# A Mamba-2 and HGRN2 trunk: SSD chunks in backs and fronts, silu as one operation, the last tiles squared in two steps

## The chip, the cores and the metric

The kernel runs on one core of a Trainium2 chip. The metric is the device time of one execution in microseconds (us). The core's engines are PE (matrix products and transposes), DVE (vectors), ACT (functions of single elements, copies), POOL (little used here) and SP (which issues transfers). Each takes its instructions in a fixed order and waits on semaphores for the others.

## The reference

One step of a trunk of two layers for 1024 new frames and 32 frames of a running stream, with 1024 channels. The first layer is an SSD mixer, the second an HGRN2 mixer, and each is followed by a SwiGLU network; every part begins with an RMS norm, and one ends the whole. The change touches the first norm, the SSD mixer and the last norm. Of the mixer:

```python
def ssd_mixer(h, conv_buf, ssm_state, in_w, conv_w, conv_b, dt_bias, A_log, D_skip, gnorm_w, out_w):
    proj = h @ in_w
    z = proj[..., :SSD_D_INNER]
    xbc = proj[..., SSD_D_INNER:SSD_D_INNER + SSD_CONV_DIM]
    dt_raw = proj[..., SSD_D_INNER + SSD_CONV_DIM:]
    ...
    xbc = jax.nn.silu(acc)          # acc: causal convolution of xbc over 4 frames
    ...
    y, S = ssd_scan(xs, dt, A, Bm, Cm, ssm_state.astype(jnp.float32))
    y = y + D_skip.astype(jnp.float32)[:, None] * xs
    yg = y.reshape(Bsz, L, SSD_D_INNER) * jax.nn.silu(z.astype(jnp.float32))
    yg = yg * lax.rsqrt(jnp.mean(yg * yg, axis=-1, keepdims=True) + NORM_EPS)   # over groups of 512
    ...
    out = yg.astype(h.dtype) @ out_w
```

The scan goes over chunks of frames. With the decay from frame s to frame t of a chunk, it adds (C_t . B_s) x decay x dt_s x_s over s (the chunk's own part) to C_t . S x decay (the part of the state S), and then carries S on.

## The kernel before

Frames are columns, channels are the 128 partitions. The 1056 frames are worked on as two halves, h = 0 (512 frames) and h = 1 (544, with the running stream's 32 at the end). All products in f32 are made of three: a weight tile "raw" is split into wh (ACT copy, L118) and wl (DVE, raw minus wh, L121), and `product` (L346 to L348) multiplies wh by the input's high part, wh by its low part, and wl by its high part, for each of eight tiles of channels. So PE's third matmul of a product needs wl.

The SSD layer runs over eight units (h, g), g being one of four groups of eight heads. For a unit, `conv_tile` makes six tiles: a product into an "mm" bank of PSUM (one of 512 columns in the first half, two of 272 in the second), the bias copy "pre" on ACT, four taps (the first, "ca", on ACT, three on DVE at L124), and silu as a * (1 + tanh(a)), the halved input being in the weights: Tanh on ACT ("cth"), then one operation on DVE. `ssd_dt` makes the time steps and decays of a half ("dt" tiles: Exp, Ln, Exp on ACT, among them a scan at L514), and `ssd_cols` turns them with 9 transposes in all (L543), each copied by DVE.

`ssd_chunk` handles one of the layer's 36 chunks (four in a unit of the first half, five in one of the second): PE makes C.B (L620), four transposes of x (L625), B's transpose (L641), the state's part y2 (L648), the state's new part pp (L651) and the chunk's own part y1 (L662), each in a bank of the "sc" pool, which has three; the "mm" pool has five. ACT makes the decays "dec" (Relu, Exp), DVE multiplies and adds. After the last chunk, `ssd_gate` ends the unit: on DVE D times x, then times z; on ACT the squares "sq"; on PE their sum (L369); on ACT rstd (Ln, then Exp); on DVE Y by rstd, and then its split, yh on ACT and yl on DVE.

`ssd_layer` (L715) feeds the chunks: after each chunk stands a quarter of the unit's "tasks" (the previous unit's output products, the z products, small vectors), the first four ahead of chunk 0 (`PRE`), and behind `ssd_gate` the next unit's six conv tiles (`late`). In the first unit these are mixed with five `seconds`, each of which squares a tile of the input's second half on ACT, transposes it on PE (L212) and copies it as residual on ACT or DVE. A scheduler then sets the order on each engine from priorities and its own reckoning of when an operation is ready; only what `keep` records stays in the order of the program, as in `first_norm` (L389). ACT loads a table ("ACT_TABLE_LOAD") wherever the next function isn't in the one that is loaded.

The end is `finish_last`: the last product's tiles m = 0 to 7 are accumulated one by one; `first` transposes, squares and scales the tiles 0 to 3 of two groups of 128 frames after m = 5, `second` tiles 4 to 7 after m = 7 (L1380), and then come the root (`finish_rstd`, L1394), the scaling and four stores.

## Time and profile before

| What | us |
| --- | --- |
| three runs | 2847.61, 2849.42, 2850.42 |
| median | 2849.42 |
| the profiled execution | 2848.86 |
| its span on the engines | 2846.9 |

The profiled execution begins and ends 2.0 us around its span; times within it count from the span's start. Its TensorE clock was granted at 1.00 in the windows shown below. In the lines to come, a window's line gives the window, its length, and the busy time of PE, PEld (weight loads, beside PE's matmuls), DVE, ACT and POOL with their instructions, then the clock, the DMA engines' share and GB/s. A wait's line gives the engine and line that waited, whom for, and the total, the number and the longest. A line of the timeline gives start, duration, engine, line, operation, tiles out<-in, sizes and number, and in brackets the engine's idle time before it and who ended it. Matmuls overlap, so their pace is read from start to start.

### The profile page before, as it was taken

The page shows a single profiled execution, that of the slowest core. Times are in us where ns is not written, and L with a number is a line of the kernel's source. Part 1 is how long each engine was busy: PE and PEld are TensorE (multiplying, and loading weights), DVE is VectorE, ACT ScalarE, POOL GpSimd, SP SyncE. Part 2 cuts the span into 40 slices and gives each one's busy share as a digit, 9 for nine tenths or more (in the row PEclk, how much of TensorE's full clock was granted, in tenths as well). Part 3 has the DMA queues.
Part 4 walks back from the last instruction along what each step waited for, and adds up shares of the span by engine and source line. Part 5 has one row for each costly group of instructions (what it writes and reads, how often), then busy time and mean ns, then how long its engine had stood idle before and what let it go on. Part 6 is the DMA issues. An engine that isn't in the chain of part 4 may idle for free.

```text
span 2846.9 us, 48830 instructions
## 1 busy us (share of the span) xinstructions
PE 2824.4 (99%) x19676; PEld 2609.6 (92%) x19676; DVE 2131.0 (75%) x3663; ACT 1561.8 (55%) x2846; POOL 44.5 (2%) x158
## 2 busy tenths in 40 slices
PE   8999999999999999999999999999999999999998
PEld 8777788999989999999999888999989999999998
DVE  7887887787787877797777557655668877787776
ACT  6665554564644654565544666566644554455544
POOL 0000010010000000000000000000000000000000
PEclk9999999999999999999999999999999999999999
DMA  7434344444322432333233222222232333333322
GB/s 190 115 108 115 91 109 105 115 113 106 105 83 88 126 95 91 112 89 105 90 97 105 75 74 74 76 80 80 74 89 91 113 95 92 120 97 104 110 91 69
DMA packets 394516, 281.54 MB, mean 99 GB/s; under 512 B 16289, under 2 KB 382514, under 8 KB 394290
## 3 DMA queue, kind: packets, MB, share of 16 engines
q1 hardware_dynamic: 394274, 278.42, 33.9%
q8 instruction: 154, 2.52, 0.4%
q14 instruction: 72, 0.59, 0.1%
q10 hardware_dynamic: 16, 0.00, 0.0%
HBM read 270.57 MB, written 7.82 MB: 98 GB/s over the span
## 4 chain that ended last, share of the span: by engine, by line
PE 91%; DVE 4%; ACT 2%; DMA 1%; issue 1%; SPq 0%; POOL 0%; DVEq 0%; ACTq 0%; POOLq 0%
PE mm L346 19%; PE mm L347 19%; PE mm L348 19%; PE mm L1177 5%; PE mm L1175 5%; PE mm L1176 5%; PE sc L1177 4%; PE sc L1175 4%; PE sc L1176 4%; PE sc L662 1%; PE sc L651 1%; PE sc L648 1%; PE mm L1451 1%; DVE fixed L121 1%; ACT wh L118 1%
## 5 line engine op out<-in xcount | busy, mean ns | idle before, releaser
L118 ACT ACTIVATE wh<-raw 128x512 fp32r<-128x512 f32 (+1 forms) x687 | 554.8, 816 | 592.0 <-PE mm L347 475.9
L346 PE MATMUL mm<-xn,wh 128*128 128x272 f32 (+2 forms) x1552 | 522.2, 337 | 2.0 <-ACT pre L118 2.0
L348 PE MATMUL mm<-xn,wl 128*128 128x272 f32 (+2 forms) x1552 | 515.9, 333 | 0.9 <-DVE wl L121 0.9
L347 PE MATMUL mm<-xn,wh 128*128 128x272 f32 (+2 forms) x1552 | 515.6, 333 | 0.0
L121 DVE TENSOR_TENSOR wl<-raw,wh 128x1024 fp32r<-128x1024 f32 (+1 forms) x307 | 372.9, 1217 | 144.6 <-ACT wh L118 120.4
L121 DVE TENSOR_TENSOR fixed<-mm,fixed 128x272 f32<-128x272 f32 (+3 forms) x504 | 259.2, 525 | 180.6 <-PE mm L348 173.7
L347 PE MATMUL mm<-fl,wh 128*128 128x272 f32 (+1 forms) x992 | 322.5, 326 | 0.0
L346 PE MATMUL mm<-fh,wh 128*128 128x272 f32 (+1 forms) x992 | 322.5, 326 | 0.0
L348 PE MATMUL mm<-fh,wl 128*128 128x272 f32 (+1 forms) x992 | 322.3, 325 | 0.0
L346 PEld LDWEIGHTS mm<-xn,wh 128*128 128x128 f32 x1552 | 291.4, 188 | 31.9 <-issue 3.0
L348 PEld LDWEIGHTS mm<-xn,wl 128*128 128x128 f32 x1552 | 291.6, 188 | 30.4 <-issue 1.8
L347 PEld LDWEIGHTS mm<-xn,wh 128*128 128x128 f32 x1552 | 291.9, 188 | 27.6 <-issue 1.2
L121 DVE TENSOR_TENSOR wh<-raw,wh 128x512 fp32r<-128x512 f32 x380 | 256.4, 686 | 48.5 <-ACT wh L118 45.9
L1175 PE MATMUL mm<-th,wh 128*128 128x272 f32 (+1 forms) x912 | 261.2, 286 | 0.8 <-ACT s L118 0.8
L1177 PE MATMUL mm<-th,wh 128*128 128x272 f32 (+1 forms) x912 | 260.1, 285 | 0.2 <-DVE wh L121 0.2
L1176 PE MATMUL mm<-tl,wh 128*128 128x272 f32 (+1 forms) x912 | 259.5, 285 | 0.0
L346 PEld LDWEIGHTS mm<-fh,wh 128*128 128x128 f32 x992 | 186.1, 188 | 16.0 <-ACT fh L118 1.6
L348 PEld LDWEIGHTS mm<-fh,wl 128*128 128x128 f32 x992 | 186.6, 188 | 15.4
L347 PEld LDWEIGHTS mm<-fl,wh 128*128 128x128 f32 x992 | 186.5, 188 | 14.9 <-DVE fl L121 0.2
L1175 PEld LDWEIGHTS mm<-th,wh 128*128 128x128 f32 x912 | 171.7, 188 | 2.9 <-ACT s L118 2.2
L1175 PE MATMUL sc<-xn,wh 128*128 128x272 f32 (+1 forms) x608 | 172.9, 284 | 0.5 <-ACT wh L118 0.5
L1177 PE MATMUL sc<-xn,wh 128*128 128x272 f32 (+1 forms) x608 | 173.0, 285 | 0.0
(313 smaller groups left out, 6648.8 us busy)
## 6 DMA issues: line engine op xcount, KB each, us to landing
raw<-in_ffn_w_gate_dram SPq DMA_DIRECT2D x88, 512.0 KB, 3.8
...
```

The source lines that it names most:

```text
L118: keep(A.activation(out=out, in_=in_, func=f, **kw))
L121: keep((eng or V).tensor_tensor(out=out, in0=a, in1=b, op=op))
L346: PE.matmul(ps[:, :bn], a, mh, start=(k == 0), stop=False)
L347: PE.matmul(ps[:, :bn], a, ml, start=False, stop=False)
L348: PE.matmul(ps[:, :bn], b, mh, start=False, stop=(k == n - 1))
L648: PE.matmul(y23[:, j, :n], S[:, j * P:(j + 1) * P], Cx, start=True, stop=True)
L651: PE.matmul(pp, Btok[:n, :], xw[:n, :], start=True, stop=True)
L662: PE.matmul(y13[r:r + 64, i // 2, :n], xdt[:n, i * 64:(i + 1) * 64], cums[i // 4][:n, i % 4, :n], start=True, stop=True)
L1175: PE.matmul(ps[:, :n], a, mh, start=(k == 0 and not more), stop=False, skip_group_check=True)
L1176: PE.matmul(ps[:, :n], a, ml, start=False, stop=False, skip_group_check=True)
L1177: PE.matmul(ps[:, :n], b, mh, start=False, stop=(k == 3), skip_group_check=True)
L1451: PE.matmul(ps[:, :bn], a, x[:, b0:b0 + bn], start=i == 0, stop=i == len(ts_) - 1)
```

## The change

- `first_norm` transposes the norm weights and copies them before the input tiles are turned.
- `ssd_dt` has its first tile in the tag "s" in place of "ys".
- `ssd_cols` is gone; its transposes and copies stand in the fronts of units with g = 0.
- `ssd_chunk` becomes `ssd_front` (C.B, the transposes of B and x in two "mm" banks, the decays) and `ssd_back` (y2, pp and y1 in "sc" banks, the state). In each round of `ssd_layer` the back of chunk c - 1 comes first, then the front of chunk c, then tasks; three tasks (`LEAD`) stand ahead of the first front.
- `conv_tile` ends the tiles of the six units with g > 0 by Silu on ACT, with scale 2, and no DVE operation behind it.
- `finish_last` has a step `most` after m = 6, which transposes, squares and multiplies tiles 4 to 6, so that `second` has one tile of 128 columns left in each group.

In the two new functions and the loop of `ssd_layer`, the lines taken out (those of `ssd_chunk` and of the loop, above) are not shown again.

```diff
-        turned = [[x_turned(xs[0], q, psum_mm) for q in range(2)], [x_turned(xs[1], 0, psum_mm)]]
         ps = psum_sc()
         keep(PE.transpose(ps[:, :8], rows[:8, :], ident[:8, :8]))
+        keep(V.tensor_copy(vc[:, C_SSDN:C_SSDN + 8], ps[:, :8]))
+        turned = [[x_turned(xs[0], q, psum_mm) for q in range(2)], [x_turned(xs[1], 0, psum_mm)]]
         banks = [psum_sc() for _ in range(3)] + [psum_mm()]
         ds = [diagonals(c, c + 1)[0] for c in range(2)]
-        keep(V.tensor_copy(vc[:, C_SSDN:C_SSDN + 8], ps[:, :8]))
         ws = [wsplit(w0, KD)]
...
-        e, v, u, ln, t = [T("ys", "dt") for _ in range(5)]
+        e, v, u, ln, t = [T(k, "dt") for k in ("s", "ys", "ys", "ys", "ys")]
...
-    def ssd_cols(h):
-        pk, _, elast = dts[h]
-        cols = colt[:, :5 * P].rearrange("p (c t) -> p c t", t=P)
-        for c, (o, n, _) in enumerate(CHUNKS[h]):
-            ps = psum_sc()
-            PE.transpose(ps[:n, :P], pk[:, o:o + n], ident)
-            V.tensor_copy(cols[:n, c, :], ps[:n, :P])
-        dts[h] = cols, elast
...
+        if silu:
+            act(a[:, :W], a[:, :W], AF.Silu, scale=2.0)
+            return a
         th = T("w", "cth")
         act(th[:, :W], a[:, :W], AF.Tanh)
         stt(a[:, :W], th[:, :W], 1.0, a[:, :W], ADD, MUL)
...
+    def ssd_front(h, g, c, loads, u):
         o, n, smp = CHUNKS[h][c]
+        Bt, Ct, xs = u["x"][0], u["x"][1], u["x"][2:]
+        pk, cols, elast = dts[h]
         xo = o + (3 if smp else 0)
         Bx, Cx = Bt[:, xo:xo + n], Ct[:, xo:xo + n]
         h0 = g * 8
         cums, ec = loads
+        ps, px = psum_mm(), psum_mm()
         PE.matmul(ps[:n, :n], Bx, Cx, start=True, stop=True)
+        PE.transpose(ps[:n, P:2 * P], Bx, ident)
+        if not g:
+            PE.transpose(ps[:n, 2 * P:3 * P], pk[:, o:o + n], ident)
+            V.tensor_copy(cols[:n, c, :], ps[:n, 2 * P:3 * P])
+        for j in range(4):
+            PE.transpose(px[:n, j * P:(j + 1) * P], xs[j][:, xo:xo + n], ident)
+        cbm, Btok = small("cbm"), small("Btok")
         tt(cbm[:n, :n], ps[:n, :n], cmask[:n, :n], MUL)
+        act(Btok[:n, :], ps[:n, P:2 * P], AF.Copy)
+        x3 = px[:n, :].rearrange("p (h q) -> p h q", q=64)
         xdt, xw = T("xd", "xdt")[:, :512], T("xd", "xw")[:, :512]
+        for t, k in ((xdt, 0), (xw, 64)):
+            tt(t[:n, :].rearrange("p (h q) -> p h q", q=64), x3,
+               cols[:n, c, k + h0:k + h0 + 8].unsqueeze(2).to_broadcast([n, 8, 64]), MUL)
+        decs = []
         for q in range(2):
             cb3 = T("de", "dec")[:, :512].rearrange("p (h t) -> p h t", t=P)
             for i in range(4):
                 hh = 32 + h0 + 4 * q + i
                 act(cb3[:n, i, :n], cums[q][:n, i, :n], AF.Relu, scale=-1.0, bias=cols[:n, c, hh:hh + 1])
             act(cb3[:n, :, :n], cb3[:n, :, :n], AF.Exp, scale=-1.0)
             tt(cb3[:n, :, :n], cb3[:n, :, :n], cbm[:n, :n].unsqueeze(1).to_broadcast([n, 4, n]), MUL)
+            decs.append(cb3)
+        return decs, ec, xdt, xw, Btok, Cx
+
+    @lifted("chunk")
+    def ssd_back(h, g, c, S, made, u):
+        o, n, smp = CHUNKS[h][c]
+        decs, ec, xdt, xw, Btok, Cx = made
+        elast = dts[h][2]
+        h0 = g * 8
+        quads = "p (j t) -> p j t"
         if ec is not None:
+            y2 = psum_sc().rearrange(quads, t=P)
             for j in range(4):
+                PE.matmul(y2[:, j, :n], S[:, j * P:(j + 1) * P], Cx, start=True, stop=True)
+            tt(ec[:, :, :n], y2[:, :, :n], ec[:, :, :n], MUL)
+            S3 = S.rearrange("p (h q) -> p h q", q=64)
+            tt(S3, S3, elast[:, h0:h0 + 8, c:c + 1].to_broadcast([P, 8, 64]), MUL)
+        pp, y1 = psum_sc(), psum_sc().rearrange(quads, t=P)
         PE.matmul(pp, Btok[:n, :], xw[:n, :], start=True, stop=True)
+        for i in range(8):
+            r = 64 * (i % 2)
+            PE.matmul(y1[r:r + 64, i // 2, :n], xdt[:n, i * 64:(i + 1) * 64], decs[i // 4][:n, i % 4, :n],
+                      start=True, stop=True)
+        yo = u["Y"][:, :, o:o + n]
         if ec is None:
             V.tensor_copy(S, pp)
+            act(yo, y1[:, :, :n], AF.Copy)
         else:
             tt(S, S, pp, ADD)
+            tt(yo, y1[:, :, :n], ec[:, :, :n], ADD)
...
-        return [lambda ct=ct: u["x"].append(conv_tile(h, ct, xns[h], blocks or BLK[h], ws.get(ct))) for ct in order]
+        return [lambda ct=ct: u["x"].append(conv_tile(h, ct, xns[h], blocks or BLK[h], ws.get(ct), g > 0)) for ct in order]
...
-                ssd_cols(h)
+                dts[h] = dts[h][0], colt[:, :5 * P].rearrange("p (c t) -> p c t", t=P), dts[h][2]
...
+            run(tasks[:LEAD])
+            tasks = tasks[LEAD:]
+            made = None
+            for c in range(nch + 1):
+                if c:
+                    ssd_back(h, g, c - 1, Ss if CHUNKS[h][c - 1][2] else Sst[g], made, u)
+                if c < nch:
+                    made = ssd_front(h, g, c, loads, u)
+                if c + 1 < nch:
+                    loads = chunk_loads(h, g, c + 1, False)
+                if c < nch:
+                    q = -(-len(tasks) // (nch - c))
+                    run(tasks[:q])
+                    tasks = tasks[q:]
...
+        last, Q = [], 3 * P
+
+        def turned(g, ps, js):
+            for k, j in enumerate(js):
+                PE.transpose(ps[:, k * P:(k + 1) * P], acc[g[0]][4 + j][:, g[1]:g[1] + P], ident)
+
+        def squared(yo, ps, dst):
+            act(yo, ps, AF.Square, accum_out=dst)
+
+        def most():
+            for g, ss in zip(groups, sums):
+                ps, yo = psum_sc(), T("w", "yo")[:, :512]
+                turned(g, ps, range(3))
+                squared(yo[:, :Q], ps[:, :Q], ss[:, 1:2])
+                tt(ss[:, 0:1], ss[:, 0:1], ss[:, 1:2], ADD)
+                tt(yo[:, :Q], ps[:, :Q], wrow[1][:, :Q], MUL)
+                last.append(yo)
+
         def second():
-            last = [finish_half(g, 1, ss, psum_sc, "w") for g, ss in zip(groups, sums)]
-            for g, ss, y0, (ps, yo) in zip(groups, sums, yos, last):
-                n = g[2]
+            ps = psum_sc()
+            tiles = [ps[:, i * P:(i + 1) * P] for i in range(len(groups))]
+            for g, t in zip(groups, tiles):
+                turned(g, t, (3,))
+            for ss, yo, t in zip(sums, last, tiles):
+                squared(yo[:, Q:], t, ss[:, 1:2])
+            for g, ss, y0, yo, t in zip(groups, sums, yos, last, tiles):
                 r = finish_rstd(g, ss)
-                stt(yo[:n, :], ps[:n, :], r, wrow[1][:n, :], MUL, MUL)
-                act(y0[:n, :], y0[:n, :], AF.Copy, scale=r)
+                act(y0, y0, AF.Copy, scale=r)
                 finish_out(g, 0, y0)
+                V.tensor_scalar_mul(yo[:, :Q], yo[:, :Q], r)
+                stt(yo[:, Q:], t, r, wrow[1][:, Q:], MUL, MUL)
                 finish_out(g, 1, yo)
-        return first, second
+        return first, most, second
...
-        first, second = finish_last(groups_of(h, 0, 256))
+        first, most, second = finish_last(groups_of(h, 0, 256))
         later = groups_of(h, 256, LEN[h])
         mid = {m: lambda g=g: finish(g) for m, g in zip((0, 2, 4), later)}
-        mid[5] = first
+        mid[5], mid[6] = first, most
```

The scheduler's order moves with it. Three places follow; a number in a name tells apart tiles of one kind, and the same tile has other numbers before and after.

ACT at the boundary of the first unit to the second, before: "wh_1462" is the weight copy of the second unit's fifth conv tile, "sq<-fixed" squares of the input's second half, "yh<-Y" the first unit's split.

```order
L118 ACTIVATE wh_1462<-raw_1460 128x1024
L118 ACT_TABLE_LOAD
L118 ACTIVATE rstd_1199<-sc_1200,fixed 128x512
L118 ACT_TABLE_LOAD
L118 ACTIVATE cth_1264<-ca_1259 128x512
L118 ACTIVATE rstd_1199<-rstd_1199 128x512
L118 ACTIVATE sq_1267,fixed<-fixed 128x512
L118 ACTIVATE sq_1269,fixed<-fixed 128x512
L118 ACTIVATE yh_1205<-Y_801 128x512
L118 ACTIVATE fixed<-sc_1277 128x4x128
L118 ACTIVATE yh_1210<-Y_801 128x512
L118 ACTIVATE pre_1289<-mm_1291 128x512
```

The copy wh_1462 stands ahead of the two table loads. ACT at the same place now, from the bias copy pre_1336 of the third conv tile:

```order
L118 ACTIVATE pre_1336<-mm_1338 128x512
L118 ACTIVATE sq_1373,fixed<-fixed 128x512
L118 ACTIVATE ca_1365<-pre_1336,fixed 128x512
L118 ACTIVATE dec_1670<-cumB_1545,fixed 128x128 x2
L118 ACT_TABLE_LOAD
L118 ACTIVATE dec_1670<-dec_1670 128x512
L118 ACT_TABLE_LOAD
L118 ACTIVATE rstd_1191<-sc_1192,fixed 128x512
L118 ACTIVATE fixed<-sc_1267 128x4x128
L118 ACT_TABLE_LOAD
L118 ACTIVATE rstd_1191<-rstd_1191 128x512
L118 ACT_TABLE_LOAD
```

and two rows further on, to the weight copy wh_1446, which the fifth conv tile's product mm_1452 on PE reads:

```order
L118 ACTIVATE fixed<-sc_1324 128x4x128
L118 ACTIVATE fixed<-sc_1381 128x4x128
L118 ACTIVATE yh_1202<-Y_789 128x512
L118 ACTIVATE sq_1428,fixed<-fixed 128x512
L118 ACTIVATE yh_1207<-Y_789 128x512
L118 ACTIVATE ca_1365<-ca_1365 128x512
L118 ACTIVATE sq_1430,fixed<-fixed 128x512
L118 ACTIVATE yh_1212<-Y_789 128x512
L118 ACTIVATE pre_1393<-mm_1395 128x512
L118 ACTIVATE fixed<-sc_1438 128x4x128
L118 ACTIVATE ca_1422<-pre_1393,fixed 128x512
L118 ACTIVATE wh_1446<-raw_1444 128x1024
```

Four table loads, Exp, Ln and two silu ("ca<-ca") now stand between pre_1336 and wh_1446; the two rows left out between the fences are the silu of ca_1308 and yh_1197. On PE, the matmuls of the fourth tile (mm_1395), the sum at L369 and 40 transposes of L212 stand between mm_1338, the third tile's product, and mm_1452.

DVE at the start of the second half, where the unit (0, 3) ends, before: "wl_3887" and "wl_3959" are the low weights of the next unit's second and third conv tiles, "Y<-Y,fixed,rstd" the scaling of the ended unit.

```order
L121 TENSOR_TENSOR sq_3776<-sq_3776,sq_3778 128x512
L127 TENSOR_SCALAR dt_3687<-mm_3691,fixed 128x272
L121 TENSOR_TENSOR sq_3776<-sq_3776,sq_3781 128x512
L127 TENSOR_SCALAR dt_3687<-mm_3718,fixed 128x272
L121 TENSOR_TENSOR sq_3776<-sq_3776,sq_3784 128x512
L505 TENSOR_SCALAR dt_3688<-dt_3686 128x544
L121 TENSOR_TENSOR wl_3887<-raw_3884,wh_3886 128x1024
L124 SCALAR_TENSOR_TENSOR dt_3686<-dt_3688,dt_3686 128x544
L121 TENSOR_TENSOR wl_3959<-raw_3956,wh_3958 128x1024
L124 SCALAR_TENSOR_TENSOR Y_3140<-Y_3140,fixed,rstd_3787 128x512 x3
L121 TENSOR_TENSOR yl_3794<-Y_3140,yh_3793 128x512
L124 SCALAR_TENSOR_TENSOR Y_3140<-Y_3140,fixed,rstd_3787 128x512
```

They stand ahead of the scaling. The same place now, "wl_3903" being the third conv tile's:

```order
L124 SCALAR_TENSOR_TENSOR ca_3820<-pre_3762,fixed,ca_3820 128x547
L124 SCALAR_TENSOR_TENSOR Y_3088<-Y_3088,fixed,rstd_3731 128x512 x3
L121 TENSOR_TENSOR yl_3738<-Y_3088,yh_3737 128x512
L124 SCALAR_TENSOR_TENSOR Y_3088<-Y_3088,fixed,rstd_3731 128x512
L121 TENSOR_TENSOR yl_3743<-Y_3088,yh_3742 128x512
L121 TENSOR_TENSOR dt_3610<-dt_3610,dt_3611 32x544
L121 TENSOR_TENSOR yl_3748<-Y_3088,yh_3747 128x512
L124 SCALAR_TENSOR_TENSOR ca_3820<-pre_3762,fixed,ca_3820 128x547
L121 TENSOR_TENSOR yl_3753<-Y_3088,yh_3752 128x512
L124 SCALAR_TENSOR_TENSOR ca_3820<-pre_3762,fixed,ca_3820 128x547
L121 TENSOR_TENSOR wl_3903<-raw_3900,wh_3902 128x1024
L121 TENSOR_TENSOR wl_3975<-raw_3972,wh_3974 128x1024
```

The low weights come behind all scalings and splits of Y and behind the three taps of the first tile. PE, at the place where it first needs them, has these rows now ("L771" turns a state, wh_3902 and wl_3903 are of the third tile, wh_3974 of the fourth):

```order
L346 MATMUL mm_3909<-xn,wh_3902 128x272
L347 MATMUL mm_3909<-xn,wh_3902 128x272
L346 MATMUL mm_3935<-xn,wh_3902 128x272
L347 MATMUL mm_3935<-xn,wh_3902 128x272
L771 MATMUL sc_4192<-fixed,sr_4190 128x128 x4
L346 MATMUL mm_3981<-xn,wh_3974 128x272
L348 MATMUL mm_3909<-xn,wl_3903 128x272
L346 MATMUL mm_3909<-xn,wh_3902 128x272
L347 MATMUL mm_3909<-xn,wh_3902 128x272
```

The products mm_3909 and mm_3935 of the third tile are begun with wh alone, then the fourth tile's is begun, and then PE needs wl_3903.

DVE at the end, before: "fixed<-mm" is an accumulate of 256 columns, the fifth row that of m = 7.

```order
L121 TENSOR_TENSOR fixed<-mm_30496,fixed 128x256
L121 TENSOR_TENSOR yo_30515<-mm_30510,fixed 128x512
L121 TENSOR_TENSOR yo_30523<-mm_30518,fixed 128x512
L121 TENSOR_TENSOR fixed<-mm_30527,fixed 128x256
L121 TENSOR_TENSOR fixed<-mm_30541,fixed 128x256
L121 TENSOR_TENSOR fixed<-fixed 128x1 x2
L1394 RECIPROCAL fixed<-fixed 128x1
```

The last accumulate stands right behind those before it. Now, with "yo" the products of the early squares:

```order
L121 TENSOR_TENSOR fixed<-mm_30379,fixed 128x256
L121 TENSOR_TENSOR yo_30398<-mm_30393,fixed 128x512
L121 TENSOR_TENSOR yo_30406<-mm_30401,fixed 128x512
L121 TENSOR_TENSOR fixed<-mm_30410,fixed 128x256
L121 TENSOR_TENSOR fixed<-fixed 128x1
L121 TENSOR_TENSOR yo_30425<-sc_30424,fixed 128x384
L121 TENSOR_TENSOR fixed<-fixed 128x1
L121 TENSOR_TENSOR yo_30433<-sc_30432,fixed 128x384
L121 TENSOR_TENSOR fixed<-mm_30440,fixed 128x256
L121 TENSOR_TENSOR fixed<-fixed 128x1 x2
```

Two products of 384 columns, which need ACT's squares of the same tiles, now stand ahead of the accumulate of mm_30440, the last.

More of the change, by code (lines that the diff above doesn't have):

```diff
@@ L536, in ssd_dt, with conv_tile @@
         return pk, None, elast
-    def ssd_cols(h):
-        pk, _, elast = dts[h]
-        cols = colt[:, :5 * P].rearrange("p (c t) -> p c t", t=P)
-        for c, (o, n, _) in enumerate(CHUNKS[h]):
-            ps = psum_sc()
-            PE.transpose(ps[:n, :P], pk[:, o:o + n], ident)
-            V.tensor_copy(cols[:n, c, :], ps[:n, :P])
-        dts[h] = cols, elast
     def conv_w_unit(ct):
         return wraw([(0, P, ssd_in_w[0][:, DI + ct * P:DI + (ct + 1) * P])], KD)
-    def conv_tile(h, ct, xn, blocks, w=None):
+    def conv_tile(h, ct, xn, blocks, w, silu):
         L = LEN[h]
@@ L610, in ssd_chunk @@
     @lifted("chunk")
-    def ssd_chunk(h, g, c, S, loads, u):
+    def ssd_front(h, g, c, loads, u):
         o, n, smp = CHUNKS[h][c]
-        Bt, Ct, xs, Y = u["x"][0], u["x"][1], u["x"][2:], u["Y"]
-        cols, elast = dts[h]
+        Bt, Ct, xs = u["x"][0], u["x"][1], u["x"][2:]
+        pk, cols, elast = dts[h]
         xo = o + (3 if smp else 0)
@@ L618, in ssd_chunk @@
         cums, ec = loads
-        ps = psum_sc()
+        ps, px = psum_mm(), psum_mm()
         PE.matmul(ps[:n, :n], Bx, Cx, start=True, stop=True)
-        cbm = small("cbm")
+        PE.transpose(ps[:n, P:2 * P], Bx, ident)
[5 more added lines that the diff above has]
+        cbm, Btok = small("cbm"), small("Btok")
         tt(cbm[:n, :n], ps[:n, :n], cmask[:n, :n], MUL)
-        ps = psum_sc()
-        for j in range(4):
-            PE.transpose(ps[:n, j * P:(j + 1) * P], xs[j][:, xo:xo + n], ident)
-        x3 = ps[:n, :].rearrange("p (h q) -> p h q", q=64)
+        act(Btok[:n, :], ps[:n, P:2 * P], AF.Copy)
+        x3 = px[:n, :].rearrange("p (h q) -> p h q", q=64)
         xdt, xw = T("xd", "xdt")[:, :512], T("xd", "xw")[:, :512]
-        tt(xdt[:n, :].rearrange("p (h q) -> p h q", q=64), x3,
-           cols[:n, c, h0:h0 + 8].unsqueeze(2).to_broadcast([n, 8, 64]), MUL)
-        tt(xw[:n, :].rearrange("p (h q) -> p h q", q=64), x3,
-           cols[:n, c, 64 + h0:64 + h0 + 8].unsqueeze(2).to_broadcast([n, 8, 64]), MUL)
+        for t, k in ((xdt, 0), (xw, 64)):
+            tt(t[:n, :].rearrange("p (h q) -> p h q", q=64), x3,
+               cols[:n, c, k + h0:k + h0 + 8].unsqueeze(2).to_broadcast([n, 8, 64]), MUL)
+        decs = []
         for q in range(2):
@@ L636, in ssd_chunk @@
                 act(cb3[:n, i, :n], cums[q][:n, i, :n], AF.Relu, scale=-1.0, bias=cols[:n, c, hh:hh + 1])
-            cums[q] = cb3
             act(cb3[:n, :, :n], cb3[:n, :, :n], AF.Exp, scale=-1.0)
             tt(cb3[:n, :, :n], cb3[:n, :, :n], cbm[:n, :n].unsqueeze(1).to_broadcast([n, 4, n]), MUL)
-        ps = psum_sc()
-        PE.transpose(ps[:n, :P], Bx, ident)
-        Btok = small("Btok")
-        act(Btok[:n, :], ps[:n, :P], AF.Copy)
+            decs.append(cb3)
+        return decs, ec, xdt, xw, Btok, Cx
@@ L644, in ssd_chunk @@
+    @lifted("chunk")
[5 more added lines that the diff above has]
+        quads = "p (j t) -> p j t"
         if ec is not None:
-            y2 = psum_sc()
-            y23 = y2.rearrange("p (j t) -> p j t", t=P)
+            y2 = psum_sc().rearrange(quads, t=P)
             for j in range(4):
-                PE.matmul(y23[:, j, :n], S[:, j * P:(j + 1) * P], Cx, start=True, stop=True)
@@ L649, in ssd_chunk @@
-            tt(ec[:, :, :n], y23[:, :, :n], ec[:, :, :n], MUL)
-        pp = psum_sc()
-        PE.matmul(pp, Btok[:n, :], xw[:n, :], start=True, stop=True)
+                PE.matmul(y2[:, j, :n], S[:, j * P:(j + 1) * P], Cx, start=True, stop=True)
[3 more added lines that the diff above has]
+        pp, y1 = psum_sc(), psum_sc().rearrange(quads, t=P)
@@ L657, in ssd_chunk @@
             tt(S, S, pp, ADD)
-        y1 = psum_sc()
-        y13 = y1.rearrange("p (j t) -> p j t", t=P)
-        for i in range(8):
-            r = 64 * (i % 2)
-            PE.matmul(y13[r:r + 64, i // 2, :n], xdt[:n, i * 64:(i + 1) * 64], cums[i // 4][:n, i % 4, :n],
-                      start=True, stop=True)
-        yo = Y[:, :, o:o + n]
-        if ec is None:
-            act(yo, y13[:, :, :n], AF.Copy)
-        else:
-            tt(yo, y13[:, :, :n], ec[:, :, :n], ADD)
+            tt(yo, y1[:, :, :n], ec[:, :, :n], ADD)
@@ L706, in trunk_kernel @@
     PRE = 4
+    LEAD = 3
     def ssd_new_unit():
@@ L777, in ssd_layer @@
             loads = chunk_loads(h, g, 0, h == 0)
-            for t in tasks[:PRE]:
-                t()
-            tasks = tasks[PRE:]
-            for c, (o, n, smp) in enumerate(CHUNKS[h]):
-                nxt = chunk_loads(h, g, c + 1, False) if c + 1 < nch else None
-                ssd_chunk(h, g, c, Ss if smp else Sst[g], loads, u)
-                loads = nxt
-                q = -(-len(tasks) // (nch - c))
-                for t in tasks[:q]:
-                    t()
-                tasks = tasks[q:]
+            run(tasks[:LEAD])
[12 more added lines that the diff above has]
+                    tasks = tasks[q:]
             if h:
```

2 lines of the change are left out of this document (removed).

## Prediction

> **What bounds the kernel now.** I read the page first, for the busiest engine and the chain that ended last.
>
> ```profile
> PE 2824.4 (99%) x19676; PEld 2609.6 (92%) x19676; DVE 2131.0 (75%) x3663; ACT 1561.8 (55%) x2846; POOL 44.5 (2%) x158
> ...
> PE 91%; DVE 4%; ACT 2%; DMA 1%; issue 1%; SPq 0%; POOL 0%; DVEq 0%; ACTq 0%; POOLq 0%
> ```
>
> PE is busy for 2824.4 of 2846.9 us, and the change leaves PE as many matmuls and transposes as it had. So the whole case lies in some 22 us in which PE does nothing: the change can win from these, and it can add to them. The windows tell where they are.
>
> ```profile
> 0.00:40.00 40.00, 34.40 (x249) 32.45 (x250) 25.75 (x75) 26.81 (x54) 3.08 (x14) 1.00 0.82 225
> ...
> 80.00:120.00 40.00, 39.53 (x240) 30.38 (x239) 34.22 (x69) 26.40 (x61) 0.50 (x2) 1.00 0.40 109
> ...
> 500.00:860.00 360.00, 360.00 (x2738) 334.37 (x2737) 288.34 (x460) 202.47 (x414) 19.87 (x71) 1.00 0.41 107
> sum 860.00, PE 849.94 PEld 743.05 DVE 690.32 ACT 495.37 POOL 44.51; mean PE 106.24 PEld 92.88 DVE 86.29 ACT 61.92 POOL 5.56
> 394.00:412.00 18.00, 17.10 (x132) 16.40 (x131) 15.78 (x26) 12.83 (x21) 5.78 (x8) 1.00 0.32 92
> 412.00:430.00 18.00, 17.13 (x135) 16.60 (x133) 15.26 (x20) 9.68 (x19) 1.45 (x8) 1.00 0.92 228
> ```
>
> The first number after the length is PE's busy time, the third DVE's, the fourth ACT's. In the 860 us that hold the SSD layer PE idles 10.1 us (860.00 - 849.94); 5.6 of these are in the first 40 us, 0.5 near the end of the first unit (80 to 120), 1.8 where the second half begins (394 to 430), none after 500. The waits name them.
>
> ```profile
> PE sc L405 <- DVE fixed L400: 0.7, 1, 0.7
> PE mm L346 <- ACT pre L118: 1.5, 1, 1.5
> PE sc L369 <- DVE sq L121: 0.5, 1, 0.5
> PE mm L348 <- DVE wl L121: 0.9, 1, 0.9
> PE sc L543 <- ACT pre L118: 0.9, 2, 0.5
> PE sc L435 <- DVE fixed L385: 0.7, 1, 0.7
> ```
>
> So in the steady chunks nothing can be won: PE never waits there. Grouping a chunk's matmuls into a back and a front saves PE nothing, since the same number run at the same pace.
>
> **The start.** With the norm weights copied first, the third "sc" bank is free before L405 needs it: the wait of 0.7 goes, **-0.7 us**, and everything behind it in the chain shifts. The weights' DMA and the 8-column transpose were early enough already, so nothing is late next. Bounds: 0, if xs[1]'s first product finds the next late operand, to -1.7, if the next wait, L435's of 0.7, goes with it. I take -0.9.
>
> **The turned time steps.** The 9 transposes of L543 leave their own place for the fronts of units with g = 0; their waits go, 0.9 in the row above: 0.4 in the first half, **-0.4**, and 0.5 in the second, which I count below with the whole stretch 394 to 430.
>
> **The chunks.** 0, with bounds of -1 (x's transposes reach their readers earlier) and +3: a front now takes two "mm" banks, of five, from the products, so that a product could wait for DVE or ACT to empty one. DVE is busy 288.34 of 360 us in these stretches, which covers that.
>
> **The silu.** 36 conv tiles lose DVE's last operation and end on ACT with Silu instead of Tanh: no more ACT operations than before, but Silu is of another table than Exp and Ln, so the order has 132 table loads where 111 were.
>
> ```profile
> L118 ACT ACT_TABLE_LOAD x111 | 142.4, 1283 | 26.9 <-DVE fixed L849 23.7 <-PEq L1517 1.4
> ```
>
> 21 x 1.283 = 27 us more on an engine that is busy 55%. What matters is where they stand, and that is the boundary from the first unit to the second. The order shows there, between the bias copy pre_1336, which PE's mm_1338 releases, and the weight copy wh_1446, which PE needs for mm_1452, four table loads and 21 other operations. Before, the weight copy at that place stood ahead of the loads. Their paces, start to start, from the timeline of the same boundary:
>
> ```profile
> 115.95 1.28 ACT L118 ACT_TABLE_LOAD   x1
> 117.25 0.69 ACT L118 ACTIVATE rstd<-sc,fixed 128x512 f32<-128x512 f32 x1
> ...
> 120.93 0.61 ACT L118 ACTIVATE sq<-fixed 128x512 f32<-128x512 f32 x1
> ...
> 121.54 0.61 ACT L118 ACTIVATE yh<-Y 128x512 fp32r<-128x512 f32 x1
> 122.06 0.57 ACT L118 ACTIVATE fixed<-sc 128x512 f32<-128x512 f32 x1
> ...
> 123.06 0.57 ACT L118 ACTIVATE pre<-mm 128x512 f32<-128x512 f32 x1
> 123.54 1.04 ACT L118 ACTIVATE wh<-raw 128x1024 fp32r<-128x1024 f32 x1
> ...
> 125.01 0.80 ACT L118 ACTIVATE ca<-pre,fixed 128x512 f32<-128x512 f32 x1
> 125.72 1.05 ACT L118 ACTIVATE wh<-raw 128x1024 fp32r<-128x1024 f32 x1
> ```
>
> A load takes 1.30, a square with its sum 0.61, yh or silu 0.52, a copy from PSUM 0.48, a ca 0.71, a weight copy 1.05 to its end. After pre_1336 (0.48): square 0.61, ca 0.71, two small Relus 0.6, then around four loads (5.2) Exp 0.6, Ln 0.7, a copy 0.6 and Exp 0.6, which makes 10.1; then four yh and two silu 3.1, three copies 1.4, two squares 1.2, pre 0.5, ca 0.7 and the weights 1.05, another 8.0. ACT needs **18.1 us**. PE has in the same stretch 24 matmuls of 512 columns, the sum over squares at L369, and 40 transposes:
>
> ```profile
> 107.75 0.40 PE L346 MATMUL mm<-xn,wh 128*128 128x512 f32 x1
> 107.98 0.39 PE L347 MATMUL mm<-xn,wh 128*128 128x512 f32 x1
> ...
> 115.77 1.10 PE L369 MATMUL sc<-sq,fixed 128*128 128x512 f32 x2 [0.47 <-DVE sq L121]
> 116.70 1.04 PE L212 MATMUL sc<-fixed 128*128 128x128 f32 x8
> 117.50 0.48 PE L348 MATMUL mm<-xn,wl 128*128 128x512 f32 x1
> ```
>
> 24 x 0.23 + 0.93 + 40 x 0.10 = 10.5 us. PE stands 18.1 - 10.5 = 7.6 us; and its third matmul needs wl, which DVE makes from wh in 1.2 us while PE has two matmuls (0.46): +0.8. Before, PE stood 0.5 here. That is +7.9. ACT also waits for DVE in this stretch, which the sum leaves out (yh for a Y that DVE has yet to scale, silu for the last tap): with one wait of 0.7 for each of two of them and 0.4 for DVE's operation ahead of wl it is +9.7. I take **+8.5**, with ends of +5 (some operations ready earlier, the copies shorter) and +11.
>
> A rule of the Trainium skill bears on this: "ScalarE: Activation LUTs", section "What ACT_TABLE_LOAD costs", has 1283 ns for the load and some 1380 ns more of draining for every switch. The rows agree with the first and show nothing of the second: the load at 115.95 ends at 117.23 and Ln starts at 117.25. By the page's sum four loads would cost 5.5 us more here, and the forecast would be near 2872; I give that 3 in 100, inside the rival of more stalls.
>
> **The second half's start.** The unit there (h = 1, g = 0) keeps its Tanh, but DVE's order changes: before, the weights wl_3887 and wl_3959 of the next two conv tiles stood ahead of the last Y operations; now wl_3903, of the third tile, stands behind all of them, behind the dt work and behind two of the conv taps. PE's order shows nothing in between to fill with: two matmuls each of two products, four transposes, one more. DVE's paces:
>
> ```profile
> 386.13 1.41 DVE L124 SCALAR_TENSOR_TENSOR Y<-ca,fixed,Y 128x512 f32<-128x512 f32 x2
> 387.45 1.29 DVE L121 TENSOR_TENSOR Y<-Y,z 128x512 f32<-128x512 f32 x2
> ...
> 399.25 2.08 DVE L124 SCALAR_TENSOR_TENSOR Y<-Y,fixed,rstd 128x512 f32<-128x512 f32 x3 [2.10 <-ACT rstd L118]
> 401.25 0.69 DVE L121 TENSOR_TENSOR yl<-Y,yh 128x512 fp32r<-128x512 f32 x1
> ...
> 403.15 0.78 DVE L124 SCALAR_TENSOR_TENSOR ca<-pre,fixed,ca 128x547 f32<-128x547 f32 x1
> ...
> 407.88 1.27 DVE L514 TENSOR_TENSOR_SCAN dt<-fixed,dt 128x544 f32<-128x544 f32 x1
> 409.08 1.19 DVE L121 TENSOR_TENSOR wl<-raw,wh 128x1024 fp32r<-128x1024 f32 x1
> ```
>
> From the last y1: its own Y 0.6, eight Y operations 5.0, three sums of squares 1.8, four Y by rstd 2.7, four yl 2.4, three ca 2.1, the scan 1.2, nine other dt operations 3.4, wl 1.2: 20.4 us. PE has until then 100 matmuls of 272 columns, the sum at L369 and four transposes:
>
> ```profile
> 394.30 0.29 PE L346 MATMUL mm<-xn,wh 128*128 128x272 f32 x1
> 394.42 0.29 PE L347 MATMUL mm<-xn,wh 128*128 128x272 f32 x1
> ```
>
> 100 x 0.125 + 0.9 + 0.4 = 13.8 us. So PE stands at least 6.6 us. Besides, DVE waits: the rstd now stands on ACT behind a dt Exp that needs the scan, and has two loads, so DVE has 2 us of nothing there, as it had 2.10 before; ahead of Y it waits for a dt step behind two loads, up to 2.6; and the yh add some 2: 13.4 us at most. Less the 1.8 us of before: +4.8 to +11.6, and I take **+8**, near the middle.
>
> **Other boundaries.** The same sums, ACT against PE, leave PE covered from unit 1 to 2 and 2 to 3, and short by about 1 us at one of the three in the second half: **+0.8** (0 to +4).
>
> **The end.** The early squares of three of the four last tiles put two DVE products that wait for them ahead of the last accumulate, which took place here:
>
> ```profile
> 2838.60 0.43 DVE L121 TENSOR_TENSOR fixed<-mm,fixed 128x256 f32<-128x256 f32 x1 [0.20 <-PE mm L1451]
> 2840.17 0.16 DVE L121 TENSOR_TENSOR fixed<-fixed 128x1 f32<-128x1 f32 x1 [1.14 <-ACT yo L118]
> ```
>
> Transposes after the accumulate at 2838.00 to 2838.40 (0.7), the two squares (some 0.5 each) and the products put it at about 2840.7, 2 us late; the shorter last squares (128 columns for 512) and the products done earlier win about 0.9 back. **+1.1**, from -0.7 (the accumulate is on time) to +2.
>
> **Sum.** -0.9 - 0.4 + 8.5 + 8 + 0.8 + 1.1 = +17.1, on the profiled run's own 2848.86 us (a span of 2846.9 and 2.0 around it; the median of the runs, 2849.42, is 0.6 above): **2866 us**.
>
> **Rivals.** A measurement of this kernel tells 0.2%, 5.7 us, from no change.
> - Both boundaries stall as summed: 2856 to 2876. Chance 0.64. For it: four engines' orders are fixed, and ACT is released there by PE itself.
> - More stalls: loads at the five other boundaries with silu uncovered (three more each, 3.9 us, if half of them show, +10), or products waiting for banks in the 36 chunks: 2876 to 2886. Chance 0.14. Against it: ACT is busy 202.47 of 360 us in the second half's chunks.
> - The stalls are mostly covered, because ACT and DVE reach these places sooner, DVE with an operation less in each of 36 tiles: the bounds at their low ends and the start's gain, 2849 to 2855: same. Chance 0.14.
> - Faster. The place is ACT's queue behind pre_1336: if the weight copy wh_1446 is reached within PE's 10.5 us, nothing is added, and what goes is the start (-1.7), L346's wait of 1.5, L543's 0.9 and the 1.3 left at 394 to 430: -5.4, with the end on time -6.1, about 2843. Chance 0.08. Against it: the 18.1 us are serial.
> - That the change does not do what it says: PE's idle time stays at 22 us and the end is where it was; it is in the third.
>
> The range runs from 2852 to 2878. Faster 0.08, same 0.14, slower 0.78.
>
> **What would show it.** PE waiting some 8 us in all for wh and wl of mm_1452's tile, near 120 to 135, and again for wl and L369 near 395 to 410; PE busy time unchanged at about 2824; 132 loads; L405's wait gone; the last accumulate 2 us after the matmuls. It is wrong if PE shows no wait of over 3 us at either boundary, or if stalls appear inside the chunks.

## The result and the profile after

The changed kernel takes 2870.18 us (median of six runs, 2869.76 to 2872.34) beside 2850.48 us of the kernel before in its six runs: a ratio of 1.0071, with a 95% interval of 1.0061 to 1.0082. It is slower by 19.7 us; the forecast was 17.1 more, 2866 us.

The page after, engines and chain (the profiled execution's span is 2868.4 us):

```profile
PE 2826.2 (99%) x19676; PEld 2613.0 (91%) x19676; DVE 2106.5 (73%) x3633; ACT 1592.2 (56%) x2871; POOL 80.9 (3%) x158
...
PE 91%; DVE 4%; ACT 3%; DMA 1%; issue 1%; POOL 0%; SPq 0%; ACTq 0%; DVEq 0%; POOLq 0%
```

PE does its work in 2826.2 us, 1.8 more than before, and is idle for 2868.4 - 2826.2 = 42.2 us where it was 22.5. DVE has 24.5 us less to do and ACT 30.4 more, and neither number shows in the time. The windows after, in the columns described above:

```profile
0.00:40.00 40.00, 34.73 (x270) 33.37 (x271) 28.10 (x79) 29.25 (x59) 3.49 (x16) 1.00 0.81 225
40.00:80.00 40.00, 40.00 (x246) 35.24 (x244) 31.94 (x44) 24.46 (x49) 1.42 (x10) 1.00 0.56 139
80.00:112.00 32.00, 31.71 (x195) 23.32 (x194) 29.38 (x63) 23.87 (x59) 2.21 (x3) 1.00 0.48 126
112.00:144.00 32.00, 23.46 (x111) 18.43 (x112) 22.39 (x36) 24.26 (x41) 3.69 (x10) 0.89 0.26 82
144.00:390.00 246.00, 246.00 (x1253) 196.68 (x1252) 182.42 (x264) 142.07 (x255) 15.94 (x25) 1.00 0.39 105
390.00:440.00 50.00, 37.32 (x271) 35.15 (x270) 37.63 (x58) 28.44 (x46) 11.68 (x16) 0.86 0.29 79
440.00:860.00 420.00, 418.91 (x3224) 389.05 (x3223) 312.19 (x507) 239.57 (x497) 42.50 (x79) 1.00 0.40 107
```

Before, between 40 and 80 us and in the two windows that matter most:

```profile
40.00:80.00 40.00, 38.05 (x246) 34.08 (x245) 31.38 (x45) 23.50 (x44) 1.63 (x10) 1.00 0.57 140
...
112.00:144.00 32.00, 31.53 (x154) 25.07 (x153) 26.77 (x38) 23.62 (x40) 1.29 (x6) 1.00 0.34 100
...
390.00:440.00 50.00, 48.14 (x343) 45.05 (x342) 44.28 (x68) 34.45 (x64) 8.86 (x24) 1.00 0.51 132
```

Most of the loss sits in two windows: at the first boundary PE idles 8.5 us where it idled 0.5, at the second half's start 12.7 where it was 1.9. That is 18.9 us of the 19.7 by which PE's idle time grew; smaller gains and losses stand beside it. The granted clock, third number from the end, falls to 0.89 and 0.86 in the same two windows and is 1.00 in the other five. Between 144 and 390 us, where most of the first half's chunks run, PE misses nothing, and missed 0.2 us before. The first 80 us are better by 2.3 us of idle time. The waits of PE after, with total, number and longest:

```profile
PE mm L346 <- ACT wh L118: 14.4, 3, 8.3
PE mm L348 <- DVE wl L121: 5.2, 4, 3.0
PE sc L369 <- DVE sq L121: 2.6, 2, 1.4
```

PE waits for the two halves of its weights. In the kernel before it waited at L346 to L348 for a low half once, 0.9 us, and never for a high one. ACT's timeline shows the first of the two places:

```profile
111.28 0.60 ACT L118 ACTIVATE pre<-mm 128x512 f32<-128x512 f32 x1 [0.67 <-PE mm L348]
...
113.79 1.28 ACT L118 ACT_TABLE_LOAD   x1
...
115.74 1.28 ACT L118 ACT_TABLE_LOAD   x1
117.03 0.69 ACT L118 ACTIVATE rstd<-sc,fixed 128x512 f32<-128x512 f32 x1
...
118.22 1.28 ACT L118 ACT_TABLE_LOAD   x1
...
120.17 1.28 ACT L118 ACT_TABLE_LOAD   x1
121.46 0.63 ACT L118 ACTIVATE ca<-ca 128x512 f32<-128x512 f32 x1
...
128.43 1.05 ACT L118 ACTIVATE wh<-raw 128x1024 fp32r<-128x1024 f32 x1
```

From pre at 111.28, which PE released, to the end of wh at 129.48, ACT works without a gap for 18.2 us; the sum in the prediction was 18.1. The loads at 115.74 and 120.17 are followed within 0.02 us by the next operation, and the one at 115.74 starts 0.02 us behind the end of the Exp ahead of it (115.09 + 0.63), so no time to drain shows on either side of it. Here the trace goes against the rule of the Trainium skill that was weighed (ScalarE: Activation LUTs, What ACT_TABLE_LOAD costs). PE's timeline at the end of that wait:

```profile
129.54 0.80 PE L346 MATMUL mm<-xn,wh 128*128 128x512 f32 x1 [5.70 <-ACT wh L118]
...
132.33 0.79 PE L348 MATMUL mm<-xn,wl 128*128 128x512 f32 x1 [1.56 <-DVE wl L121]
132.92 0.63 PE L346 MATMUL mm<-xn,wh 128*128 128x512 f32 x1
133.34 0.63 PE L347 MATMUL mm<-xn,wh 128*128 128x512 f32 x1
...
135.36 0.39 PE L346 MATMUL mm<-xn,wh 128*128 128x512 f32 x1
135.59 0.39 PE L347 MATMUL mm<-xn,wh 128*128 128x512 f32 x1
```

PE stood 0.46 us for an earlier wl and 1.11 for L369 on the way there, so up to wh it stood 7.3 us, where the sum had 7.6. The wait for wl behind it is longer than summed, 1.56 us for 0.8, because DVE has two taps (1.45 us) ahead of that copy:

```profile
129.60 1.53 DVE L124 SCALAR_TENSOR_TENSOR ca<-pre,fixed,ca 128x512 f32<-128x512 f32 x2
131.05 1.22 DVE L121 TENSOR_TENSOR wl<-raw,wh 128x1024 fp32r<-128x1024 f32 x1
```

What the sum had not: the matmuls from 132.92 follow each other by 0.42 us, those from 135.36 by 0.23. After standing for some 6 us PE comes back at about half pace, which costs some 1.8 us up to 135.4. The second place, PE and then DVE:

```profile
408.84 1.13 PE L369 MATMUL sc<-sq,fixed 128*128 128x512 f32 x2 [1.45 <-DVE sq L121]
...
419.65 0.60 PE L346 MATMUL mm<-xn,wh 128*128 128x272 f32 x1 [8.27 <-ACT wh L118]
423.22 0.60 PE L348 MATMUL mm<-xn,wl 128*128 128x272 f32 x1 [2.97 <-DVE wl L121]
423.62 0.43 PE L346 MATMUL mm<-xn,wh 128*128 128x272 f32 x1
423.84 0.43 PE L347 MATMUL mm<-xn,wh 128*128 128x272 f32 x1
```

```profile
414.65 2.08 DVE L124 SCALAR_TENSOR_TENSOR Y<-Y,fixed,rstd 128x512 f32<-128x512 f32 x3 [1.98 <-ACT rstd L118]
...
421.25 0.78 DVE L124 SCALAR_TENSOR_TENSOR ca<-pre,fixed,ca 128x547 f32<-128x547 f32 x1
421.95 2.35 DVE L121 TENSOR_TENSOR wl<-raw,wh 128x1024 fp32r<-128x1024 f32 x2
```

PE stands 1.45 + 8.27 + 2.97 = 12.7 us; the most that the prediction's sum allowed was 13.4. The longest of the three waits is for the fourth tile's wh, which ACT makes behind rstd and the yh; the sum didn't name it. PE's next matmul in order needs the third tile's wl, which came last, so it is wl that fixed the end of the stall. DVE comes to the low weights at 421.95, behind all of the ended unit's work, after 1.98 us without work for rstd. Then 272 columns go at 0.22 us in place of 0.125, up to 428.3: 22 matmuls, some 2.2 us.

### The profile page after: what moved, and what is told of

It reads as the page before. It is cut to its first block, busy times and chain, and to the rows that moved or that the text cites. A ratio compares the mean times of both kernels' runs of the same rounds, so it can differ in the third digit from the quotient of the medians.

```text
span 2868.4 us, 48871 instructions
## 1 busy us (share of the span) xinstructions
PE 2826.2 (99%) x19676; PEld 2613.0 (91%) x19676; DVE 2106.5 (73%) x3633; ACT 1592.2 (56%) x2871; POOL 80.9 (3%) x158
## 4 chain that ended last, share of the span: by engine, by line
PE 91%; DVE 4%; ACT 3%; DMA 1%; issue 1%; POOL 0%; SPq 0%; ACTq 0%; DVEq 0%; POOLq 0%
PE mm L346 19%; PE mm L348 19%; PE mm L347 19%; PE mm L1179 5%; PE mm L1177 5%; PE mm L1178 5%; PE sc L1179 4%; PE sc L1177 4%; PE sc L1178 4%; PE sc L658 1%; PE sc L655 1%; PE sc L650 1%; ACT L118 1%; PE mm L1476 1%; DVE fixed L121 1%
## 5 line engine op out<-in xcount | busy, mean ns | idle before, releaser
L346 PE MATMUL mm<-xn,wh 128*128 128x272 f32 (+2 forms) x1552 | 521.0, 336 | 14.8 <-ACT wh L118 14.4
L348 PE MATMUL mm<-xn,wl 128*128 128x272 f32 (+2 forms) x1552 | 518.5, 335 | 5.3 <-DVE wl L121 5.2
L121 DVE TENSOR_TENSOR fixed<-mm,fixed 128x272 f32<-128x272 f32 (+3 forms) x540 | 268.7, 506 | 191.0 <-PE mm L348 181.9
L346 PEld LDWEIGHTS mm<-xn,wh 128*128 128x128 f32 x1552 | 293.3, 189 | 43.9 <-ACT wh L118 14.9
L348 PEld LDWEIGHTS mm<-xn,wl 128*128 128x128 f32 x1552 | 293.1, 189 | 36.9 <-DVE wl L121 7.2
L346 PE MATMUL mm<-fh,wh 128*128 128x272 f32 (+1 forms) x992 | 322.9, 326 | 1.5 <-DVE fixed L121 1.5
L348 PE MATMUL mm<-fh,wl 128*128 128x272 f32 (+1 forms) x992 | 322.7, 326 | 0.0
L346 PEld LDWEIGHTS mm<-fh,wh 128*128 128x128 f32 x992 | 186.3, 188 | 17.7 <-DVE fixed L121 2.0
L348 PEld LDWEIGHTS mm<-fh,wl 128*128 128x128 f32 x992 | 186.6, 188 | 15.3
L1179 PE MATMUL sc<-xn,wh 128*128 128x272 f32 (+1 forms) x608 | 172.9, 284 | 0.0
```

The source lines that it names most:

```text
L121: keep((eng or V).tensor_tensor(out=out, in0=a, in1=b, op=op))
L346: PE.matmul(ps[:, :bn], a, mh, start=(k == 0), stop=False)
L348: PE.matmul(ps[:, :bn], b, mh, start=False, stop=(k == n - 1))
L1179: PE.matmul(ps[:, :n], b, mh, start=False, stop=(k == 3), skip_group_check=True)
```

## The experiments

The two stalls are plain in the trace. Open were the cause of each (the silu, the split into fronts and backs, or the number of table loads), and the size of the small terms. Each run stands beside executions of the kernel before that were timed together with it, whose medians were 2849.12 (e1 to e3), 2849.99 (e4 to e7), 2850.13 (e8, e9) and 2849.56 us (e10, e11).

### e1: no silu

```diff
-... conv_tile(h, ct, xns[h], blocks or BLK[h], ws.get(ct), g > 0)
+... conv_tile(h, ct, xns[h], blocks or BLK[h], ws.get(ct), False)
```

> The kernel after, with Tanh and DVE's last operation back in all six units (111 table loads plus two); fronts, backs, the start and the end stay new. Theory (the loss is two queues at two unit boundaries, whose order the silu operations upset): PE waits under 2 us at each of the two places, the granted clock stays at 1.00 there, and the time is 2846 to 2850 us. Rival A (the split into backs and fronts is what costs): 2862 us or more. Rival B (the second boundary has no silu in its own unit, so its 13 us stay): about 2860 us.

Measured: 2849.54 us, ratio 1.0003 (0.9993 to 1.0012). The time is as the theory had it, and rivals A and B fall: without silu both stalls shrink, the second too, though its own unit has Tanh in either kernel. The theory was wrong on what is left: a wait of 3.8 us for wl remains at the second place, where it allowed 2, and with it a clock of 0.93 where it had 1.00:

```profile
112.00:144.00 32.00, 30.86 (x152) 24.69 (x152) 27.62 (x42) 23.17 (x41) 3.80 (x7) 1.00 0.33 99
...
390.00:440.00 50.00, 46.17 (x309) 43.69 (x309) 43.14 (x62) 29.10 (x51) 10.20 (x24) 0.93 0.39 111
```

### e2: silu alone, in the kernel before

```diff
+        if silu:
+            act(a[:, :W], a[:, :W], AF.Silu, scale=2.0)
+            return a
         th = T("w", "cth")
```

> The kernel before, with Silu in the six units and nothing else new (131 table loads). Theory: the boundary of the first unit to the second stalls PE for some 8 to 11 us with a clock drop behind it, the second half's start does not; time 2858 to 2864 us. Rival A (the split costs, the loads are hidden): 2849 to 2852 us. Rival C (each table load more costs about its own 1.3 us wherever it stands): 2850 + 20 x 1.3, near 2876 us.

Measured: 2858.74 us, ratio 1.0037 (1.0024 to 1.0050), as the theory had it. PE idles 7.6 us at the first boundary, 6.3 of them in one wait for wl, and the second half's start is as in the kernel before:

```profile
112.00:144.00 32.00, 24.39 (x114) 19.00 (x113) 25.96 (x42) 26.10 (x44) 4.35 (x9) 0.84 0.22 68
390.00:440.00 50.00, 48.19 (x378) 45.96 (x377) 44.98 (x69) 28.66 (x51) 5.37 (x17) 1.00 0.45 122
```

The way is not quite that of the kernel after: here the copy that comes late is wl on DVE (126.49), behind four scalings of Y, which waited for rstd behind three table loads on ACT. So the silu makes the first stall with the fronts or without them. For the second it needs another part of the change; e4 and e5 (below) have 48.16 and 48.20 us of PE in that window at a clock of 1.00, so that it isn't the new start or the new end, and the fronts with the turned time steps and the new tag are left.

### e10 and e11: silu in the second unit alone, and in the five others alone

```diff
-... ws.get(ct), g > 0)
+... ws.get(ct), (h, g) == (0, 1))                  # e10
+... ws.get(ct), g > 0 and (h, g) != (0, 1))        # e11
```

> The kernel after with silu in the tiles of the second unit (0, 1) alone, Tanh in all others (117 table loads, six more than before). Theory (each boundary's loss comes from the silu of the unit that is made there): the first boundary stalls as in the kernel after, 8.5 us of PE idle in 112 to 144 against 1.1 in e1, with 1.4 us of slow clock behind it, and 390 to 440 is as in e1: 2849.5 + 9 = 2858 to 2859 us. Rival (loads cost by their number): 2849.5 + 4 x 1.3 = 2855 us, and no wait of over 3 us for wh.

> The kernel after with silu in the five units other than (0, 1) (128 table loads). Theory: no stall of over 2 us at 112 to 144, and the second half's start stalls as in the kernel after (12.7 us of PE idle in 390 to 440 against 3.8 in e1, and about 1.5 us more of slow clock), although the unit made there keeps its Tanh: 2849.5 + 11 = 2859 to 2862 us. Rival (loads by number): 2849.5 + 15 x 1.3 = 2869 us. Second rival (the stall at the second half's start came from the delay of the first boundary): 2849 to 2852 us.

Measured: 2860.36 us for e10 and 2860.13 for e11, both with a ratio of 1.0038. Over e1 that is 10.8 and 10.6 us; together 21.4, and the kernel after stands 20.6 over e1. The windows part cleanly, e10 first:

```profile
112.00:144.00 32.00, 23.16 (x110) 17.84 (x109) 23.32 (x37) 24.39 (x42) 3.66 (x9) 0.89 0.27 82
...
390.00:440.00 50.00, 46.20 (x346) 44.55 (x345) 41.56 (x63) 29.73 (x47) 8.59 (x16) 0.93 0.34 97
```

```profile
112.00:144.00 32.00, 31.25 (x154) 25.19 (x155) 27.62 (x41) 22.88 (x41) 3.89 (x6) 1.00 0.33 100
...
390.00:440.00 50.00, 37.33 (x273) 35.82 (x272) 40.39 (x59) 26.70 (x48) 12.21 (x20) 0.90 0.35 100
```

Four table loads more in e10 (117 for 113) cost as much as fifteen in e11 (128), so their number isn't what counts, and the second stall doesn't come from the first. e10 came 1.4 us above its expectation. Which of e11's five units brings the second stall, and why silu in other units moves the low weights back on DVE at the second half's start, was not settled: it goes through the scheduler's reckoning, of which a trace shows only the result.

### e3: the weight copies lifted

```diff
-    HP = dict(..., dt=0, wl=0, hf=0, conv=0)
+    HP = dict(..., dt=0, wl=400, hf=0, conv=0)
```

> The kernel after with one number changed: the weight copies wh and wl get a higher priority (wl=400 in the table HP), so they stand ahead of the ended unit's work at both boundaries; all silu and 133 table loads stay. Theory: PE's waits for wh and wl of 5.7 + 2.0 and 8.3 + 3.0 us fall under 2 us at each place, the clock stays up, time 2845 to 2851 us. Rival C (the loads themselves cost): 2868 us or more. A third way: the copies, being first, delay the chunks' own operations and open other waits, 2852 to 2862 us.

Measured: 2851.91 us, ratio 1.0011 (1.0001 to 1.0021). One number takes back 17 of the 19.7 us, each kernel beside its own runs of before, with 133 table loads, so rival C falls for good. It is 0.9 us over what the theory allowed and has something of the third way: both waits for weights are gone, but PE now waits 3.1 us for ACT's Ss at the second half's start. (The profiled execution, 2849.72 us, is the fastest of the ten.)

```profile
PE mm L346 <- ACT Ss L118: 3.1, 1, 3.1
PE sc L369 <- DVE sq L121: 0.7, 1, 0.7
```

### e4 and e5: the new start alone, the new end alone

e4 is the kernel before with the norm weights transposed and copied first, e5 the kernel before with `most` and the short `second`, as in the diff above.

> The kernel before with the new order in first_norm alone. Theory (the trace of the kernel after has PE at its first product 1.8 us earlier, because L405's wait is gone and the transposes run at the quick pace from about 8.5 us on): 1.5 to 3 us less, 2846 to 2848 us, L405's wait of 0.7 gone, nothing else changed. Rival (the gain at the start belongs to the other parts): within 0.7 us of before.

> The kernel before with the new finish_last alone. Theory (two products of 384 columns stand ahead of the last accumulate on DVE): the last accumulate starts 2 us later behind the last matmul and the end comes 1 to 2 us later, 2850 to 2851.5 us. Rival (the early squares shorten the end, and the 1.6 us of the kernel after come from elsewhere): 0.5 to 1 us less than before.

Measured: e4 2847.47 us, ratio 0.9991 (0.9982 to 0.9999), 2.5 us less; e5 2851.25 us, ratio 1.0003 (0.9994 to 1.0012), 1.3 us more by the medians, which the interval doesn't tell from nothing. PE's start in e4:

```profile
7.49 1.65 PE L405 MATMUL sc<-fixed 128*128 128x128 f32 x6 [0.20 <-DVE fixed L385]
...
12.71 0.36 PE L346 MATMUL mm<-xn,wh 128*128 128x256 f32 x1
```

The first product comes at 12.71 us, and came at 14.53 in the kernel before. L405's wait was 0.75 of this; the rest is pace, since the same 32 transposes of L405 that run from 7.29 to 14.17 there run from 7.49 to 12.35 here. The other profiles bear it out: the three with the old start (before, e2, e5) have the first product at 14.5 to 15.2 us, the ten with the new one at 12.2 to 13.0. For the end, DVE's timeline in e5 shows the order at work:

```profile
2838.47 0.40 DVE L121 TENSOR_TENSOR fixed<-mm,fixed 128x256 f32<-128x256 f32 x1
2839.90 0.16 DVE L121 TENSOR_TENSOR fixed<-fixed 128x1 f32<-128x1 f32 x1 [1.03 <-ACT yo L118]
2839.98 0.55 DVE L121 TENSOR_TENSOR yo<-sc,fixed 128x384 f32<-128x384 f32 x1
...
2840.51 0.55 DVE L121 TENSOR_TENSOR yo<-sc,fixed 128x384 f32<-128x384 f32 x1
2840.98 0.41 DVE L121 TENSOR_TENSOR fixed<-mm,fixed 128x256 f32<-128x256 f32 x1
```

The last accumulate follows the one before by 2.5 us, where 0.6 lay between them (2838.00 and 2838.60).

### e6 to e9: looking for a version that beats both kernels

e6 is e4 with wl=400, e9 is e6 with dt=500 too, e7 is e3 with the old end, e8 is e1 with the old end and wl=200.

> The kernel before with the new first_norm and the weight copies lifted (wl=400), without silu, fronts and the new end. Theory: the gain at the start, and the waits of 0.9 for wl near 405 and 0.5 for L369 near 115 mostly gone too: 2844 to 2847 us, the fastest of all. Rival (lifted copies push back what the next units wait for, as in e3, where PE waited 3.1 us for ACT's Ss): 2848 to 2851 us.

> The kernel after with the weight copies lifted (as e3) and the old finish_last. Theory: e3 less the 1.6 us of the end: 1 to 2 us below e3, about 2850 us; with it the split and the silu stand at no gain over before. Rival (the end costs nothing): equal to e3, 2851.9 us.

> The kernel after without silu (Tanh in all units), with the old finish_last and the weight copies lifted (wl=200): the new start, the fronts with the turned time steps, and nothing of what cost. Theory (fronts cost PE nothing, the order at the boundaries does): e1 less 1.6 us at the end and less its wait of 3.8 for wl near 410 with the clock drop behind it, 2844 to 2847 us, at or under the kernel with the new start alone. Rival (lifted weights push the dt steps back again, as in e6): 2849 us or more.

> e6 with the dt steps lifted above the weights (dt=500). Theory (e6 lost because lifted weights pushed back the dt steps, for which L543 waited 5.1 us): that wait goes and the time falls from 2855.6 to 2845 to 2848 us. Rival (lifting only changes who waits): another wait of 3 us or more at 390 to 440, and 2850 us or more.

Measured: e6 2855.57 us, ratio 1.0022 (1.0013 to 1.0031), worse than both the theory and its rival: with the weights lifted, PE waits 5.1 us in one piece at L543, for the time steps that DVE now makes behind the weights. e9, 2858.93 us, 1.0030 (1.0019 to 1.0042), showed that lifting those too only moves the loss: the wait of 5.1 at the second half's start goes, and one of 4.1 at L543 comes at the first half's, between 40 and 80 us. Its theory fell, and its rival was right on the time but not on the place. e7, 2850.95 us, 1.0003 (0.9994 to 1.0011), is 1.0 below e3, and 1.8 by each one's distance to its own runs of before, as expected, though the two intervals overlap.

e8, 2847.57 us, ratio 0.9990 (0.9981 to 0.9999), is 2.6 us under the kernel before, as fast as e4: 0.1% each. With the fronts, lifted weights cost no wait for time steps, in e8 as in e3 and e7: PE waits 1.2 us for Ss at the second half's start and 0.7 for a tap at 444 us, and the clock stays at 1.00. That the fronts do this by carrying the time steps is likely, but no run took that part out alone.

e4 has the first of the change's six parts, e8 the first four, with lifted weights; no run gained more.

## Why the prediction was right, and where its sum was not

The direction, the two places and their mechanism are as forecast: 2870.2 measured, 2866 stated, in the range of 2852 to 2878. Term by term:

- **The start, -0.9.** Mis-sized: the first product comes 1.8 us sooner, and e4 has -2.5 us by the medians, more than the bound of -1.7, though e4's interval (0.3 to 5.1 us) holds the bound too. The sum counted the wait that goes, and not that the transposes then run at the quick pace sooner.
- **The turned time steps, -0.4.** Mis-sized: 40 to 80 us has no idle time now and had 1.95. L346's wait of 1.5 for "pre" went as well, which the sum left in place; e4 and e5 still have it, e1 doesn't, so it belongs to the fronts with the time steps and their tile's new tag.
- **The chunks, 0.** Right: PE is busy for 246.00 of 246.00 us between 144 and 390.
- **The silu at the first boundary, +8.5.** Right in place and chain, and in size partly by luck: 8.5 of idle time less the 0.5 of before, and some 1.8 of slow matmuls behind it; e10 has 10.8 over e1. ACT's 18.1 us were 18.2. But the sum raised its 7.9 for waits of ACT for DVE, which did not come, since ACT had no gap; two taps of 1.45 us ahead of wl, which it hadn't counted, filled their place.
- **The second half's start, +8.** Right in place and chain (at 409 to 423 us, later than the 395 to 410 of the forecast), low in size: 10.8 us more idle time, and some 2.2 of slow matmuls. The sum followed DVE's queue and what DVE waits for; ACT's wh, for which PE stood the longest, wasn't a term, though it was made before the wl that ended the stall. I took a value near the middle of 4.8 and 11.6; the long walk (13.4; its own terms give 13.2) was nearer than the bare sum (6.6), since DVE did wait for rstd (1.98) and for the dt step (1.67). What I hadn't seen is that this stall, too, needs the silu (e1, e2, e11): the prediction treated it as a consequence of the new order without naming what in the change caused that.
- **Other boundaries, +0.8.** Near enough: 1.1 us of idle time between 440 and 860, none before.
- **The end, +1.1.** The late accumulate is in e5's rows; its price is 1.3 us by e5's median, with an interval that reaches past nothing, so the size isn't shown.
- **The pace after a stall** was no term. It is worth some 4 us, and 3.1 (1.6 and 1.5) are missing on the other side, at the start and between 40 and 80 us. The two errors nearly cancel, and that is luck; what is left of the 4.2 us is in the main the second half's start (2.8).

Of the rivals, the one of more stalls was wrong: PE idled nothing between 144 and 390 us and 1.1 us between 440 and 860, where the other boundaries and chunks are. That of the drain at a table load fell with it. Those of covered stalls, same and faster, needed ACT to reach wh_1446 sooner; ACT had no gap to give.
